# A three-branch recurrent decoder step: the row of reciprocal norms read from PSUM, and another order of the projections

## The chip, the cores and the metric

The kernel runs on one core of one Trainium2 chip. The metric is device time in microseconds (us) of one execution, and less is better. The core's engines work at the same time, each through its own instructions in order: PE (TensorE, matmuls; PEld is its weight load), DVE (VectorE), ACT (ScalarE), POOL (GpSimd) and SP (SyncE, which here only issues DMAs). Semaphores make one engine wait for another. PE writes to PSUM, which DVE and ACT can read; everything else lies in SBUF.

## The reference, cut to what matters

One layer is applied to a prompt of 2048 tokens with 16 learned tokens in front, and to 8 samples of 8 tokens (80 rows in all beside the prompt):

```
h    = rms_norm(x, norm_w)                    # x * rsqrt(mean(x*x)) * norm_w
proj = h @ w_in                               # 1024 -> 5648 + 3*1024 columns
A: q,k,v = conv(width 4) -> silu;  gated delta rule in chunks -> RMSNorm * silu(z)
B: q,k,v, input and forget gates;  mLSTM memory in chunks     -> RMSNorm * sigmoid(o) * silu(z)
C: S5: complex diagonal scan over u, gelu, GLU                -> * silu(z)
x    = x + (sum_b sigmoid(gate_b) * (branch_b @ W_b)) @ W_out
y    = rms_norm(x, final_norm_w)
```

All of it is float32, and the final states of every branch are outputs as well. Features lie on the partitions and tokens along the free dimension, so a norm is one number for each token: a row, which has to be known on all 128 partitions.

## The kernel before, in words

**Tiles.** The tokens go through in six blocks, `BLOCKS` (L30) times 128: block 0 has 336 (the 80 rows and 256 of the prompt), blocks 1 to 4 have 384, block 5 has 256. In each block every product with 128 output features is 24 matmuls: eight input chunks, and for each of them three passes (high part by high part, high by low, low by high; L199). A weight comes in two halves of 128x512 through SP's queue (L225); ACT rounds each half to its high part `wh` (L226) and DVE subtracts it for the low part `wl` (`weights`, L188 being the helper that records every such DVE operation). There are four buffers for loaded weights and three each for `wh` and `wl`.

**Steps.** A plan names the steps of a block: `R` the rows of gates (a product with a long chain of short DVE operations behind it, tiles `rX`, `rE`, `rC`, `rW`), `C` their columns, `u0` to `u3` the S5 input projections, `s0` to `s3` the S5 scans, `d0` to `d11` the delta-rule projections with their convolution, `m0` to `m11` those of the mLSTM, `p`, `I`, `N` preparations, the triangular inverse and the mLSTM gates, `M`, `g`, `D` the chunked tiles, `F` the S5 gate products of the GLU, `X0` to `X2` the branch mixes, `E` the end of the delta rule, `S` the S5 tables (block 0 only, low priority). `:1` runs a step as far as its first yield, and `!` issues the rest behind the projection then running. `PLAN0` is the plan of block 0, `PLAN` that of the others. The order in which the plan writes the steps is their priority; a scheduler then puts the instructions of each engine in order by readiness and priority, so a moved name moves work on every engine.

**Banks.** A dense product writes a bank of the PSUM pool `pd`, which has three; the next product but two takes the same bank and must wait until it has been read out. A `u` step is read out by one ACT copy (tile `s5u`), after which it goes through a DRAM buffer `us` and comes back as `s5U` for the scan. An `m` step is read out by one ACT operation. A `d` step is read by ACT twice and then by three DVE multiply-adds (`cacc`, the convolution's taps):

```
self.act(acc[:, :T], ps, AF.Copy, scale=tap(3))              # ACT reads PSUM
for j in range(3):
    self.stt(o, src(j), tap(j), o, OP.mult, OP.add)          # DVE reads PSUM
```

In block 0 the taps read a copy in SBUF instead. All other matmuls share three banks `pr` and two banks `s5`.

**The norm of block 0.** Block 0 projects before its norm is known: the products of `R` and `u0` to `u3` run on x times norm_w, and are multiplied by the row of reciprocal norms behind it. That row is a matmul of ones with a diagonal, so it is born in a `pr` bank (`self.rstd`). `norm` copies it to an SBUF tile `rb` (L359 to L362), which `rows` (one multiply) and `s5_proj` (four multiplies, the operand read with a stride) use. From the step `norm` on, block 0 uses the finished x (`xh`, `xl`). `xt` is multiplied straight by the row in PSUM.

Of the kernel before, what the change touches and what calls it, by code (L numbers as in the profile page):

```python
# [26 lines left out]
P = 128  # L27
# [4 lines left out]
TMAX = 384  # L32
# [5 lines left out]
UNITS = 12  # L38


PLAN0 = ("R u0 u1 S u2 u3 norm m8 m7 C m6 m10 m1 m0 m4 m5 d4 m9 m2 m3 d5 m11 M0 M1 M2 d0 d3 d2 s0 s1 s2 s3 d7 d8 d9 d10 d1 "
         "d6 d11 p I N X1 g0 g1 D0 D1 g2 D2 F X2 Ud E X0 Um").split()
OUT0 = ["n"] * 19 + ["o"] * 99
PLAN = ("R C u0 u1 u2 s0:1 s1:1 u3 d0 d1 s0! s2:1 m1 m0 s1! s3:1 m2 m3 s2! d6 d2 s3! d10 d3 d4 m4 m7 m6 d7 d5 m5 d8 p d9 "
        "m9 d11 M0:2 m11 M1:2 m10 m8 M0 M1 M2 F N I g0 D0 g1 D1 g2 D2 X2 X1 E X0").split()
OUT = ["n"] * 19 + ["o"] * 99


# [5 lines left out]
GROUP = {  # L54
    "rX": "rows", "rE": "rows", "rD": "rows", "rW": "rows", "rC": "rows", "rM": "rows", "rH": "rows",
    "nacc": "acc", "nsq": "wide", "cacc": "wide", "zt": "wide", "zo": "wide", "fin": "wide", "mt": "wide",
    "macc": "wide", "rb": "wide", "s5v": "raw", "s5g": "wide", "raw": "raw", "junk": "junk",
# [49 lines left out]
class Kernel:  # L107
# [219 lines left out]
    def norm(self, g):  # L327

        T, V = g.T, self.V
        xu = [self.unit([P, 4, T], name="xt") for _ in range(2)]  # L330
        xt = [xu[k // 4][:, k % 4] for k in range(8)]
        for k in range(8):
            src = self.I["xt"][k, :, g.t0:g.t0 + T]
            if g.first:
                with self.tc.high_priority(offset=5000):
                    (self.nc.sync if k % 2 else self.nc.scalar).dma_start(xt[k], src)
            else:
                self.nc.sync.dma_start(xt[k], src)
        acc = self.temp([P, TMAX], "nacc")[:, :T]
        w = lambda k: self.vec[:, V_NW + k:V_NW + k + 1]  # L340
        if g.first:

            uh, ul = ([self.unit([P, 4, T], F32R, name="xw") for _ in range(2)] for _ in range(2))
            with self.tc.high_priority(offset=4000):
                for k in range(8):
                    self.add_square(acc, xt[k], k == 0)
                    h = uh[k // 4][:, k % 4]
                    self.act(h, xt[k], AF.Copy, scale=w(k))
                    self.stt(ul[k // 4][:, k % 4], xt[k], w(k), h, OP.mult, OP.subtract)
        else:  # L350
            for k in range(8):
                self.add_square(acc, xt[k], k == 0)
        yield
        for _ in self.rstd_row(acc, g):
            yield
        rb = self.rstd
        xh, xl = ([self.xp.tile([P, 4, TMAX], F32R, name=self.name(s), tag=s, bufs=2)[:, :, :T] for _ in range(2)]
                  for s in ("xh", "xl"))
        if g.first:  # L359
            self.rb = self.temp([P, TMAX], "rb")[:, :T]  # L360
            self.A.copy(self.rb, rb)
            self.xh, self.xl = uh, ul  # L362
        self.xn = xh, xl
        for k in range(8):
            with self.tc.high_priority(offset=3000 if g.first else 0):
                self.stt(xt[k], xt[k], w(k), rb, OP.mult, OP.mult)
                self.A.copy(xh[k // 4][:, k % 4], xt[k])
                self.tt(V if g.first and k < 4 else self.G, xl[k // 4][:, k % 4], xt[k], xh[k // 4][:, k % 4], OP.subtract)
# [1057 lines left out]
    def run(self):  # L1426
# [12 lines left out]
        for b in range(len(BLOCKS)):  # L1439
# [11 lines left out]
            steps, self.live, self.mixed = self.steps(), {"O": out}, 0  # L1451
            for w in PLAN0 if self.first else PLAN:
                late = w[-1] == "!"
# [9 lines left out]
            for w in OUT0 if self.first else OUT:  # L1463
                next(out if w == "o" else norm, None)
# [109 lines left out]
```

## Time and profile before

| what | value |
|---|---|
| runs | 2762.54, 2766.62, 2773.35 us; median 2766.62 |
| profiled execution | 2762.64 us, span 2760.9 us |
| mean granted TensorE clock | 0.98 of full |
| busy | PE 2637.4 us, DVE 2020.9, ACT 1263.0, POOL 685.9 |
| blocks by PE's first matmul of `R` | 6.5, 539.4, 1006.1, 1467.7, 1931.5, 2395.0 us |

The profile is one execution. Its page lists busy times of the engines, the chain of work that ended last, and the costliest groups of instructions. Views of the trace give more: windows (busy time of each engine in a stretch), waits (for whom an engine stood idle, and how long), timelines (each instruction with the idle time ahead of it) and tiles (all instructions that touch one buffer). The span less PE's busy time is what PE stood idle, and the windows split it by block.

### The profile page before, as it was taken

The numbers are of one execution on the slowest core, as the hardware profiler recorded it, in microseconds if no ns is written. First come the engines' busy times: TensorE is split into PE (matmuls) and PEld (weight loads), VectorE is DVE, ScalarE is ACT, GpSimd is POOL, SyncE is SP. The second block draws the span as 40 slices with busy tenths as digits, with TensorE's granted clock in tenths as the row PEclk, the third lists the DMA queues.
The fourth block names the chain that finished last, engine by engine and source line by source line (L and its number), as shares of the span: only waits on it lengthen the run. The fifth ranks groups of instructions, "written<-read, shape, count | busy, mean of one in ns | idle before, by whom it ended". The sixth has DMA issues, their size and how long they took to land.

```text
span 2760.9 us, 49716 instructions
## 1 busy us (share of the span) xinstructions
PE 2637.4 (96%) x17416; PEld 2565.8 (93%) x17416; DVE 2020.9 (73%) x4458; ACT 1263.0 (46%) x2900; POOL 685.9 (25%) x852
## 2 busy tenths in 40 slices
PE   6899799999999999999999999999999999989998
PEld 5899798989999999999999999999999999979998
DVE  7889666798864589875468887456988645788765
ACT  4354343544543454553344454345445434546444
POOL 8642233211302221221221031123014022202022
PEclk8999899999999999999999999999999999999999
DMA  5635546664443455434355534335553434565544
GB/s 151 201 115 172 145 128 190 190 184 150 115 131 99 150 171 171 142 117 118 104 168 165 175 114 128 109 108 170 177 167 108 135 95 125 174 195 153 167 146 149
DMA packets 312892, 405.36 MB, mean 147 GB/s; under 512 B 118529, under 2 KB 147969, under 8 KB 312641
## 3 DMA queue, kind: packets, MB, share of 16 engines
q1 hardware_dynamic: 299760, 384.56, 46.5%
q10 hardware_dynamic: 12880, 17.62, 1.8%
q8 instruction: 137, 2.24, 0.4%
q14 instruction: 115, 0.93, 0.1%
HBM read 370.54 MB, written 31.53 MB: 146 GB/s over the span
## 4 chain that ended last, share of the span: by engine, by line
PE 64%; DVE 6%; DMA 2%; issue 1%; ACT 1%; SPq 0%; DVEq 0%; ACTq 0%
PE pd L199 55%; PE pr L199 6%; PE s L199 2%; DVE wl L188 2%; PE pr L203 1%; DVE cacc L196 1%; DVE s5a L1257 1%; DVE s5a L188 1%; DMA s5g<-ys 0%; DMA s5w<-s5w 0%; DMA s5U<-us 0%; DMA s5t<-s5p 0%; DVE h L196 0%; ACT wh L226 0%; DVE s5g L196 0%
## 5 line engine op out<-in xcount | busy, mean ns | idle before, releaser
L226 ACT CAST wh<-w 128x512 fp32r<-128x512 f32 x1092 | 674.7, 619 | 1023.2 <-PE pd L199 839.0
L188 DVE TENSOR_TENSOR wl<-w,wh 128x512 fp32r<-128x512 f32 x1092 | 814.2, 748 | 419.1 <-ACT wh L226 391.7
L199 PE MATMUL pd<-xh,wh 128*128 128x384 f32 (+2 forms) x3272 | 1077.2, 329 | 24.9 <-DVE cacc L196 13.4
L199 PE MATMUL pd<-xh,wl 128*128 128x384 f32 (+2 forms) x3272 | 1074.4, 329 | 15.3 <-DVE wl L188 14.8
L199 PE MATMUL pd<-xl,wh 128*128 128x384 f32 (+2 forms) x3272 | 1068.8, 327 | 6.4 <-DVE xl L188 6.4
L199 PEld LDWEIGHTS pd<-xh,wh 128*128 128x128 f32 x3272 | 624.8, 191 | 33.8 <-ACT wh L226 15.0
L199 PEld LDWEIGHTS pd<-xh,wl 128*128 128x128 f32 x3272 | 623.9, 191 | 26.9 <-DVE wl L188 20.6
L199 PEld LDWEIGHTS pd<-xl,wh 128*128 128x128 f32 x3272 | 624.7, 191 | 9.0 <-DVE xl L188 7.1
L188 POOL TENSOR_TENSOR macc<-macc,mt 128x384 f32<-128x384 f32 (+2 forms) x96 | 125.6, 1308 | 453.6 <-DVE mt L196 446.7
L188 POOL TENSOR_TENSOR s5a<-s5a,s5a 128x384 f32<-128x384 f32 (+2 forms) x48 | 52.4, 1106 | 599.5 <-DVE s5a L188 555.6
L199 PE MATMUL pd<-mh,wl 128*128 128x384 f32 (+2 forms) x384 | 124.6, 328 | 0.9 <-DVE wl L188 0.9
L199 PE MATMUL pd<-mh,wh 128*128 128x384 f32 (+2 forms) x384 | 124.2, 325 | 0.8 <-ACT wh L226 0.8
L199 PE MATMUL pd<-ml,wh 128*128 128x384 f32 (+2 forms) x384 | 123.2, 323 | 0.0
L196 DVE SCALAR_TENSOR_TENSOR cacc<-pd,c,cacc 128x384 f32<-128x384 f32 (+1 forms) x180 | 103.8, 583 | 0.8
L199 PE MATMUL s<-s5U,s5w 128*128 128x96 f32 (+2 forms) x576 | 87.9, 277 | 15.4 <-DMA s5U<-us 5.2
L182 POOL COPY U<-UC 32x128 f32<-32x128 f32 x68 | 22.9, 336 | 316.9 <-ACT UC L693 314.2
L196 DVE SCALAR_TENSOR_TENSOR mt<-mt,pd 128x384 f32<-128x384 f32 (+2 forms) x96 | 50.1, 522 | 68.0 <-PE pd L199 67.6
L199 PEld LDWEIGHTS s<-s5U,s5w 128*128 128x128 f32 x576 | 79.5, 194 | 20.0 <-issue 11.2
L185 ACT ACTIVATE mt<-pd,c 128x384 f32<-128x384 f32 (+2 forms) x144 | 79.4, 551 | 2.7 <-PE pd L199 2.4
L199 PEld LDWEIGHTS pd<-mh,wl 128*128 128x128 f32 x384 | 72.1, 188 | 3.6 <-DVE wl L188 3.1
L1257 DVE TENSOR_TENSOR_SCAN s5a<-s5R,s5a,s5a 128x96 f32<-128x96 f32 (+2 forms) x192 | 69.0, 419 | 7.1 <-ACT s5a L1255 6.7
L199 PEld LDWEIGHTS pd<-mh,wh 128*128 128x128 f32 x384 | 72.4, 189 | 1.9 <-ACT wh L226 1.4
(402 smaller groups left out, 4400.9 us busy)
## 6 DMA issues: line engine op xcount, KB each, us to landing
w<-in_wi_dram SPq DMA_DIRECT2D x816, 256.0 KB
w<-in_wb_dram SPq DMA_DIRECT2D x144, 256.0 KB
s5w<-s5w SPq DMA_DIRECT2D x120, 256.0 KB
w<-in_wo_dram SPq DMA_DIRECT2D x96, 256.0 KB
s5t<-s5p SPq DMA_DIRECT2D x48, 192.0 KB
w<-in_wg_dram SPq DMA_DIRECT2D x24, 256.0 KB
xt<-in_xt_dram SPq DMA_DIRECT2D x32, 192.0 KB
h<-in_xt_dram SPq DMA_DIRECT2D x8, 768.0 KB
```

Of the source, the lines that this page charges most:

```text
L182: return eng.tensor_copy(out, in_)
L185: return self.A.activation(out, in_, f, **k)
L188: return eng.tensor_tensor(out, a, b, op=op)
L196: return self.V.scalar_tensor_tensor(out, a, s, b, op0=op0, op1=op1)
L199: return self.E.matmul(out, lhsT, rhs, start=start, stop=stop, **k)
L203: return self.E.transpose(out, in_, self.ident[:n, :n])
L226: self.A.copy(h, w)
L1257: V.tensor_tensor_scan(g[:, a, 1:1 + m], self.s5R[:, 4 * f + a:4 * f + a + 1].to_broadcast([P, m]), x[:, a, 0:m], g[:, a, 0:1], OP.mult, O ...
```

## The change

First, `rb` is no longer copied: `self.rb` is the PSUM tile itself, so its group entry and the copy go, and the five multiplies of block 0 read one operand from PSUM, whose bank is held until the last of them. Second, in `PLAN0` `d4` goes ahead of `m1`, `m5` and `m3` ahead of where they were, and `N` ahead of `I`. Third, in `PLAN` the scans' first parts `s0:1`, `s1:1` go between the first projections, with `d0` and `u3` ahead of `u2`; `d3` takes the place of `m3`, which follows it, and `d6` goes behind `d4`; `X2` stands ahead of `D2`.

```
-PLAN0 = ("R u0 u1 S u2 u3 norm m8 m7 C m6 m10 m1 m0 m4 m5 d4 m9 m2 m3 d5 m11 M0 M1 M2 d0 d3 d2 s0 s1 s2 s3 d7 d8 d9 d10 d1 "
-         "d6 d11 p I N X1 g0 g1 D0 D1 g2 D2 F X2 Ud E X0 Um").split()
+PLAN0 = ("R u0 u1 S u2 u3 norm m8 m7 C m6 m10 d4 m1 m0 m5 m4 m3 m9 m2 d5 m11 M0 M1 M2 d0 d3 d2 s0 s1 s2 s3 d7 d8 d9 d10 d1 "
+         "d6 d11 p N I X1 g0 g1 D0 D1 g2 D2 F X2 Ud E X0 Um").split()
-PLAN = ("R C u0 u1 u2 s0:1 s1:1 u3 d0 d1 s0! s2:1 m1 m0 s1! s3:1 m2 m3 s2! d6 d2 s3! d10 d3 d4 m4 m7 m6 d7 d5 m5 d8 p d9 "
-        "m9 d11 M0:2 m11 M1:2 m10 m8 M0 M1 M2 F N I g0 D0 g1 D1 g2 D2 X2 X1 E X0").split()
+PLAN = ("R C u0 u1 s0:1 d0 s1:1 u3 u2 d1 s0! s2:1 m1 m0 s1! s3:1 m2 d3 m3 s2! d2 s3! d10 d4 d6 m4 m7 m6 d7 d5 m5 d8 p d9 "
+        "m9 d11 M0:2 m11 M1:2 m10 m8 M0 M1 M2 F N I g0 D0 g1 D1 g2 X2 D2 X1 E X0").split()
-    "macc": "wide", "rb": "wide", "s5v": "raw", "s5g": "wide", "raw": "raw", "junk": "junk",
+    "macc": "wide", "s5v": "raw", "s5g": "wide", "raw": "raw", "junk": "junk",
         if g.first:
-            self.rb = self.temp([P, TMAX], "rb")[:, :T]
-            self.A.copy(self.rb, rb)
+            self.rb = rb
             self.xh, self.xl = uh, ul
```

On PE, blocks 1 to 4 ran `R u0 u1 u2 u3 d0 d1 m1 m0 C m2 m3 d6 d2 d10 d3 d4 m4` with the scans in between, and now run `R u0 u1 d0 u3 u2 d1 m1 m0 C m2 d3 m3 d2 d10 d4 d6 m4`; from `d9` to the end of a block the steps come in the same order. The two swaps `N I` and `X2 D2` leave nearly every instruction where it was. Line numbers behind the copy are one less than before.

In block 0, DVE's rows at the multiplies by the norm row are these before (`rX` of `rows`, `s5u` and `s5v` of the S5 projections, `wl` of `m8` ahead, `xl` the low part of x):

```order
L188 TENSOR_TENSOR wl_229_988<-w_227_986,wh_228_987 128x512
L188 TENSOR_TENSOR rX_97_383<-rX_97_383,rb_46_210 128x336
L188 TENSOR_TENSOR s5u_118_485<-s5u_118_485,rb_46_210 128x4x84
L188 TENSOR_TENSOR s5v_126_526<-s5v_126_526,rb_46_210 128x4x84
L188 TENSOR_TENSOR s5u_216_939<-s5u_216_939,rb_46_210 128x4x84
L188 TENSOR_TENSOR xl_44_208<-xt_21_127,xh_42_206 128x336
L188 TENSOR_TENSOR wl_232_1006<-w_230_1004,wh_231_1005 128x512
```

and now:

```order
L188 TENSOR_TENSOR rX_96_381<-rX_96_381,pr_41_204 128x336
L188 TENSOR_TENSOR s5u_117_483<-s5u_117_483,pr_41_204 128x4x84
L188 TENSOR_TENSOR s5v_125_524<-s5v_125_524,pr_41_204 128x4x84
L188 TENSOR_TENSOR wl_228_986<-w_226_984,wh_227_985 128x512
L188 TENSOR_TENSOR s5u_215_937<-s5u_215_937,pr_41_204 128x4x84
L188 TENSOR_TENSOR xl_44_208<-xt_21_127,xh_42_206 128x336
L188 TENSOR_TENSOR wl_231_1004<-w_229_1002,wh_230_1003 128x512
```

The operand `rb_46` has become `pr_41`, the bank that `xt` is multiplied by, and the first `wl` of `m8` has moved behind three of the multiplies.

At the start of block 3, DVE's rows around the eight residual additions `h` of the block before were these (`wl_3517` and `wl_3520` are the halves of `d0`, `wl_3527` the first of `d1`; `rC`, `rE` are rows of `R`):

```order
L196 SCALAR_TENSOR_TENSOR rC_3438_16806<-rC_3438_16806,rW_3437_16805 64x384
L188 TENSOR_TENSOR wl_3517_17154<-w_3515_17152,wh_3516_17153 128x512
L196 SCALAR_TENSOR_TENSOR rC_3438_16806<-rC_3438_16806,rW_3437_16805 64x384
L196 SCALAR_TENSOR_TENSOR rC_3438_16806<-rC_3438_16806,rE_3435_16803 64x384 x2
L196 SCALAR_TENSOR_TENSOR h_3351_16388<-h_3351_16388,c_1_91,pr_3423_16743 128x384 x4
L196 SCALAR_TENSOR_TENSOR h_3352_16389<-h_3352_16389,c_1_91,pr_3423_16743 128x384 x4
L192 TENSOR_SCALAR rE_3439_16824<-rC_3438_16806,c_9_110 64x384
L188 TENSOR_TENSOR wl_3520_17172<-w_3518_17170,wh_3519_17171 128x512
L188 TENSOR_TENSOR wl_3527_17202<-w_3525_17200,wh_3526_17201 128x512
```

and now (`cacc_3489` is the convolution of `d0`, `wl_3518` and `wl_3521` the halves of `u2`):

```order
L188 TENSOR_TENSOR wl_3518_17160<-w_3516_17158,wh_3517_17159 128x512
L196 SCALAR_TENSOR_TENSOR rC_3437_16804<-rC_3437_16804,rW_3436_16803 64x384
L196 SCALAR_TENSOR_TENSOR cacc_3489_17047<-pd_3481_17008,c_6_105,cacc_3489_17047 128x384
L196 SCALAR_TENSOR_TENSOR rC_3437_16804<-rC_3437_16804,rE_3434_16801 64x384
L196 SCALAR_TENSOR_TENSOR cacc_3489_17047<-pd_3481_17008,c_6_105,cacc_3489_17047 128x384 x2
L196 SCALAR_TENSOR_TENSOR rC_3437_16804<-rC_3437_16804,rE_3434_16801 64x384
L196 SCALAR_TENSOR_TENSOR h_3350_16386<-h_3350_16386,c_1_91,pr_3422_16741 128x384 x4
L196 SCALAR_TENSOR_TENSOR h_3351_16387<-h_3351_16387,c_1_91,pr_3422_16741 128x384 x4
L188 TENSOR_TENSOR wl_3521_17178<-w_3519_17176,wh_3520_17177 128x512
L192 TENSOR_SCALAR rE_3438_16822<-rC_3437_16804,c_9_110 64x384
L188 TENSOR_TENSOR wl_3526_17200<-w_3524_17198,wh_3525_17199 128x512
```

The three multiply-adds of `d0`, which stood 14, 19 and 24 rows behind the first `h`, stand ahead of it, and the second half behind `h` is that of `u2`.

In block 5, ACT's rows from the eight output DMAs on (`wh_5675` is the second half of `m1`, `wh_5679` and `wh_5682` are those of `m0`, `pd_5632` is the bank of `d0`, `pd_5642` that of `d1`) were these:

```order
L1393 DMA out_yt_dram<-h_5469_26798 128x384 x4
L1393 DMA out_yt_dram<-h_5470_26799 128x384 x4
L226 CAST wh_5675_27755<-w_5674_27754 128x512
L226 CAST wh_5679_27775<-w_5678_27774 128x512
L244 COPY pd_5632_27559<-c_12_116 128x3
L244 COPY pd_5642_27607<-c_12_116 128x3
L226 CAST wh_5682_27793<-w_5681_27792 128x512
L572 COPY c_11_115<-pd_5632_27559 128x3
L185 ACTIVATE cacc_5640_27598<-pd_5632_27559,c_6_105 128x256
L572 COPY c_11_115<-pd_5642_27607 128x3
L185 ACTIVATE cacc_5650_27646<-pd_5642_27607,c_6_105 128x256
```

and now (`wh_5674` of `m1`, `wh_5678` of `m0`, `pd_5633` the bank of `u2`, `pd_5641` that of `d1`):

```order
L1392 DMA out_yt_dram<-h_5468_26796 128x384 x4
L1392 DMA out_yt_dram<-h_5469_26797 128x384 x4
L226 CAST wh_5674_27753<-w_5673_27752 128x512
L226 CAST wh_5678_27773<-w_5677_27772 128x512
L1201 COPY s5u_5640_27602<-pd_5633_27565 128x4x64
L244 COPY pd_5641_27605<-c_12_116 128x3
L571 COPY c_11_115<-pd_5641_27605 128x3
L185 ACTIVATE cacc_5649_27644<-pd_5641_27605,c_6_105 128x256
```

The operations on `d0`'s bank have gone from behind the DMAs (they stand seven rows and more ahead of them now), and one copy of `u2`'s bank stands there instead.

## Rows read from the trace of the kernel before

**Rows 1.** The page: busy us (share of the span) xinstructions.

```profile
PE 2637.4 (96%) x17416; PEld 2565.8 (93%) x17416; DVE 2020.9 (73%) x4458; ACT 1263.0 (46%) x2900; POOL 685.9 (25%) x852
```

**Rows 2.** Windows by block: stretch, length, busy us (instructions) of five engines, clock, DMA.

```profile
0.00:539.40 539.40, 483.76 (x3100) 448.92 (x3101) 413.89 (x955) 228.23 (x537) 236.54 (x382) 0.94 0.53 162
539.40:1006.10 466.70, 457.98 (x2903) 450.96 (x2902) 334.70 (x711) 213.07 (x482) 97.82 (x99) 0.99 0.46 139
1006.10:1467.70 461.60, 454.60 (x2902) 446.84 (x2901) 333.97 (x710) 213.83 (x482) 96.95 (x99) 1.00 0.47 140
1467.70:1931.50 463.80, 455.47 (x2901) 447.86 (x2900) 334.00 (x710) 214.30 (x482) 97.07 (x99) 1.00 0.46 139
1931.50:2395.00 463.50, 455.59 (x2900) 448.05 (x2899) 330.24 (x709) 212.60 (x482) 93.74 (x99) 1.00 0.46 139
2395.00:2760.90 365.90, 330.05 (x2720) 323.21 (x2718) 274.09 (x664) 180.94 (x435) 63.78 (x74) 0.96 0.55 163
```

**Rows 3.** Waits of PE, block 0: engine, line, awaited; us, times, longest.

```profile
PE pd L199 <- DVE wl L188: 11.1, 6, 5.9
...
PE pd L199 <- DVE xl L188: 6.4, 2, 6.0
...
PE pr L203 <- DVE s5X L188: 2.9, 2, 1.9
```

**Rows 4.** Tile rb: count, min/median/max ns, first and last start us.

```profile
L188 DVE TENSOR_TENSOR s5u<-s5u,rb x2: 769/1118/1467, 40.4 to 42.5; 128x336 f32<-128x336 f32 x2
L188 DVE TENSOR_TENSOR s5v<-s5v,rb x2: 1326/1388/1450, 41.1 to 51.3; 128x336 f32<-128x336 f32 x2
...
L188 DVE TENSOR_TENSOR rX<-rX,rb x1: 518/518/518, 40.0 to 40.0; 128x336 f32<-128x336 f32 x1
```

**Rows 5.** Tile xt, 30 to 45 us: one operand from PSUM.

```profile
L196 DVE SCALAR_TENSOR_TENSOR xt<-xt,c,pr x8: 559/559/565, 35.0 to 38.3; 128x336 f32<-128x336 f32 x8
```

**Rows 6.** Tile nacc, 5 to 60 us: both operands in SBUF.

```profile
L188 DVE TENSOR_TENSOR nacc<-nacc,nsq x7: 436/500/524, 11.5 to 18.6; 128x336 f32<-128x336 f32 x7
```

**Rows 7.** Timeline of POOL, 88 to 104 us: start, length, instruction, [idle before, releaser].

```profile
101.10 0.71 POOL L188 TENSOR_TENSOR s5xy<-s5t 128x8 f32<-128x8 f32 x1 [10.72 <-DVE rW L188]
```

**Rows 8.** Timeline of DVE, 128 to 141.5 us.

```profile
137.99 2.08 DVE L188 TENSOR_TENSOR Z<-ml,c 128x64 f32<-128x64 f32 x4 [6.10 <-POOL ml L188]
```

**Rows 9.** Timeline of PE, 134 to 141.5 us.

```profile
140.72 0.65 PE L199 MATMUL pd<-xh,wl 128*128 128x336 f32 x1 [5.87 <-DVE wl L188]
```

**Rows 10.** Waits of PE, blocks 1 to 4.

```profile
PE pd L199 <- DVE cacc L196: 7.8, 4, 3.6
PE s L199 <- DMA s5U<-us: 5.1, 3, 2.3
PE pd L199 <- DVE wl L188: 2.6, 7, 0.7
PE pr L203 <- DVE rX L196: 2.5, 3, 0.9
```

**Rows 11.** Windows at the start of block 3.

```profile
1467.70:1489.00 21.30, 21.30 (x130) 21.04 (x129) 16.57 (x39) 10.35 (x19) 0.00 (x0) 1.00 0.50 146
1489.00:1505.80 16.80, 15.41 (x90) 14.85 (x89) 16.43 (x34) 6.75 (x16) 0.00 (x0) 1.00 0.87 274
1505.80:1545.00 39.20, 35.51 (x214) 34.23 (x215) 38.44 (x77) 17.67 (x52) 5.75 (x4) 1.00 0.55 163
```

**Rows 12.** The page: the conv's multiply-adds.

```profile
L196 DVE SCALAR_TENSOR_TENSOR cacc<-pd,c,cacc 128x384 f32<-128x384 f32 (+1 forms) x180 | 103.8, 583 | 0.8
```

**Rows 13.** Waits of PE, block 5.

```profile
PE pd L199 <- DVE cacc L196: 5.6, 1, 5.6
...
PE s L199 <- DMA s5w<-s5w: 2.7, 2, 1.6
...
PE pd L199 <- ACT wh L226: 2.3, 1, 2.3
```

**Rows 14.** Timeline of ACT, 2414 to 2433 us.

```profile
2415.59 7.59 ACTq L1393 DMA_DIRECT2D out_yt_dram<-h  x8
```

## The prediction

> **What bounds the kernel now.** I read the page's totals first: PE is busy 2637.4 us of 2760.9, 96% [rows 1], so nothing can be won but what PE stands idle, 123.5 us. The windows by block divide it [rows 2]: each block's length less PE's busy time is 55.6 us in block 0, then 8.7, 7.0, 8.3 and 7.9, and 35.9 in block 5 (its tail included). Blocks 1 to 4, two thirds of the time, hold only 32 us of it, and the reader should see that no order of theirs can be worth more than that. In block 0 and block 5 the granted clock is 0.94 and 0.96 on average, so for part of them PE ran at 1.2 instead of 2.4 GHz.
>
> Then the waits of PE, one query for each kind of block. In blocks 1 to 4 it waited 7.8 us for `cacc`, once in each block: the convolution of `d0`, whose bank `m0` takes. It waited 5.1 us for S5's input to come back from DRAM, 2.6 for low weights and 2.5 for `rX`, the rows behind `C` [rows 10]. Block 5 has the same wait on `cacc` in one piece of 5.6 us, 2.3 us for a high weight and 2.7 for S5's weights [rows 13]. In block 0 it waited 11.1 us for low weights and 6.4 for `xl`, most of it in pieces of 5.9 and 6.0 [rows 3]. Nearly all of these end on DVE, which is the second thing to see: at the start of block 3 DVE is busy 16.43 us of 16.80 and 38.44 of 39.20, while the 21.3 us ahead leave it 4.7 idle [rows 11].
>
> **The norm row in PSUM.** The five multiplies by `rb` take 2.24, 2.78 and 0.52 us, 5.53 in all [rows 4]: two of `s5u`, two of `s5v`, one of `rX`. A multiply of 336 columns with both operands in SBUF took 0.50 us in a quiet stretch [rows 6], so four of the five are two to three times as long as the work needs. The multiply of `xt` with one operand from PSUM, same partitions and columns, took 0.56 in all eight instances, in the same crowded part [rows 5]. No row shows a strided read from PSUM. Bounds: each at 0.56 is 2.80, a gain of 2.7; each at the longest present multiply, 1.47, is 7.3, a loss of 1.8. I take 0.65 each, near [rows 5], a gain of 2.3.
>
> The Trainium skill, SBUF — State Buffer, "Who interferes with whom", says that a Vector instruction with two SBUF inputs contends with a GpSimd instruction that reads SBUF, and one with at most one SBUF input does not; the trace agrees, with 0.56 against up to 1.47 [rows 4, 5]. Against the change speaks the skill's VectorE: DVE Perf Modes, "Rules for kernel authors": copy from PSUM to SBUF first if many operations follow. Its Perfetto Trace Analysis, "Optimizing Scalar/DVE Operations", gives about 125 ns of access for PSUM against 60 for SBUF, by which five reads would lose 0.3 us (an estimate), and the sum would be 7.7 and not 10.
>
> The copy that goes was ACT's and nobody's bound. The bank held longer is one of three, until the last multiply at 51.3 us [rows 4]; I cost it at nothing, because the dense products have banks of their own and two of `pr` remain, and if a product of the S5 tables wanted the third, it would wait beside dense work. Of 2.3 us on DVE I count 2.0 on PE, since PE stands on `xl` and low weights right there [rows 3].
>
> **The order of block 0.** `m3` and `d4` come earlier and fill the two waits on `s5X`, 2.9 us [rows 3]. But what follows is bound elsewhere: POOL's long chain begins at 101.10, after 10.72 us of waiting for DVE's `rW` [rows 7]; its product `ml` is what DVE waits 6.10 us for in front of `Z` [rows 8], and behind `Z` stands the low weight that costs PE 5.87 us [rows 9]. PE arriving earlier only waits longer there, unless POOL begins earlier, and POOL begins earlier by DVE's gain. DVE gains about the 2.0 above and perhaps a little by order, so I book 0.5 for the order: 2.5 for block 0. Bounds: 6 won if `Z` no longer waits, 1 lost if the stall moves ahead into `d0`.
>
> **Blocks 1 to 4.** With `d0` ahead of `u2`, the bank that `m0` takes was last `u2`'s, read out by one ACT copy instead of a convolution; `d0`'s bank goes to `d1`, two projections after `d0`. So the 7.8 us on `cacc` go from this place. What is late next: DVE. The three multiply-adds, 3 x 0.583 = 1.75 us [rows 12], move out of the full stretch to ahead of `h`, into the 4.7 us of idle [rows 11]. They delay `h` by what does not fit between the rows, which I put at 0.8, so DVE comes out of it 1.0 us earlier in a block, and PE cannot gain more than DVE does while low weights bound it: the second half of `m0`'s weight, with a row of `rE` now in front, takes over part of the wait. I take 0.75 in each, 3.0. Bounds: all of [rows 10], 18, won; and 1.75 a block, 7, lost, if the moved convolution lands on the path.
>
> `d3` for `m3`, `m3` for `d6` and `d6` behind `d4` exchange steps of equal length (24 matmuls, two weight halves); they shift convolutions by a step and I cost them at nothing, with DVE's idle as cover. On SP's queue `u2`'s row to DRAM is issued some ten weight loads later, behind those of `m0` and `m2`; its reader `s2` comes five products after that, so I leave the 5.1 us on S5's input where it is. If that cover is gone, it doubles. `X2` ahead of `D2` and `N` ahead of `I` are worth nothing: the rows of every engine stay, or nearly.
>
> **Block 5.** Here `d0`'s readers on ACT stood behind eight output DMAs, 7.59 us of issuing [rows 14], and now they are ahead of them. `m0` needs only `u2`'s copy, which comes right behind its own first cast, so the 5.6 us go [rows 13]. The 2.3 on the high weight of `m1` stay, since that cast is still behind the DMAs. The load of S5's second weights now stands behind eight weight loads instead of six, and DVE has to bring `m0`'s second half; I give 1.1 of the 5.6 back: 4.5. Bounds: 8 won (with the 2.3 or the 2.7 also gone), 3 lost (all kept, and 2.7 doubled).
>
> **The sum.** 2.5 + 3.0 + 4.5 = 10.0 us. Against the profiled execution (span 2760.9 and 1.74 around it, 2762.64) this gives 2752.6; that execution lies 4.0 under the median of the runs, 2766.62, so a median would be 2756.6. I forecast 2755.
>
> **The rivals.** *The waits only move.* DVE is full where PE waits [rows 11], the first stall of block 0 is POOL's, and S5's loads cap each block: then only block 0's 2.0 is left, and the time is 2761 to 2765, say 2763. For it: PE's idle is small and is spread over many releasers. Against: block 5's wait hangs on ACT, which is busy only 46% [rows 1].
>
> *More goes than I book.* The waits on `cacc`, 7.8 + 5.6, go whole, `rX` 2.5 with them, and block 0 gives 6: 21.9, so 2741 to 2745, with a bit more if shorter stalls leave PE at 2.4 GHz for longer in blocks 0 and 5. For it: the bank is free by one ACT copy. Against: the full DVE.
>
> *Slower: the convolution of `d0` comes in the way.* Its 1.75 us stand ahead of `h`, and the second half of `u2`'s weight stands behind the eight `h`. If that half is not there when `u2`'s first 12 matmuls end, PE waits where it did not before. Price: 1.75 in five blocks, 8.8, and the S5 loads that shift with `u2`, 5.1 + 2.7 again, 16.6 in all, with nothing of the waits won: 2762.6 + 16.6 = 2779, by the median 2783, so 2781. It decides once `h` is delayed by more than the 1.75. For it: [rows 11], 16.43 of 16.80. Against: 4.7 us idle just ahead.
>
> *The swap in the title does nothing:* that holds in all four cases, and changes no number.
>
> **How the numbers follow.** The forecast (5 to 15 us won) has 0.50, the waits that move 0.18, the larger gain 0.22, the slower case 0.10. A measurement of this kernel can tell about 0.5%, 13.8 us, from no change: under 2752.8 is faster, above 2780.4 slower. A third of the forecast's range lies under it, 0.17, and all of the larger gain: 0.38 faster. Of the slower case 0.07 lies above. 0.55 is left for the same. The range goes from 2742, the middle of the larger gain, to 2770, which leaves most of the slower case out; the forecast's own is 2749 to 2762.
>
> **What would show it.** Multiplies by `pr` near 0.6 us, and `xl` ended for PE some 2 us earlier at 45; a wait in front of `Z` still near 6 us; no PE wait on `cacc` in front of `m0` in blocks 1 to 5, and in its place low weights of `m0` under 1 us; S5's input about 5 us as before; block lengths in the windows of 1 to 4 shorter by 0.5 to 1 us each, block 5's by 4 to 5. I am wrong if the PSUM multiplies take over 1 us, if waits on low weights in blocks 1 to 4 grow by more than `cacc` gives, or if block 0 changes by more than 6 us.

## The result, and the profile after

The changed kernel takes 2734.38 us, the median of four runs (2732.65 to 2739.41), where four of the kernel before took 2764.58 (2758.48 to 2773.35). The ratio is 0.9895, 95% interval 0.9881 to 0.9910: about 29 us by the ratio and 30 by the medians, three times the 10 that were forecast, and below the stated range. The profiled execution is the slowest of the four, 2739.41 us with a span of 2737.6, so the two traces differ by 23.3 us only.

The windows by block of the changed kernel (stretch, length, busy us and instructions of PE, PEld, DVE, ACT, POOL, granted clock, DMA share, GB/s), each from `R` to the next `R`:

```profile
0.00:539.70 539.70, 483.31 (x3101) 448.25 (x3102) 409.45 (x955) 229.75 (x536) 229.97 (x382) 0.94 0.54 162
539.70:999.80 460.10, 455.61 (x2901) 448.38 (x2901) 332.85 (x711) 213.74 (x482) 95.90 (x99) 1.00 0.47 141
999.80:1457.80 458.00, 454.26 (x2903) 446.79 (x2902) 333.11 (x710) 213.57 (x482) 95.78 (x99) 1.00 0.47 141
1457.80:1919.20 461.40, 455.51 (x2901) 448.23 (x2901) 331.78 (x710) 213.78 (x482) 95.85 (x99) 1.00 0.47 140
1919.20:2379.50 460.30, 453.84 (x2899) 446.67 (x2899) 329.30 (x709) 211.84 (x482) 93.64 (x99) 1.00 0.47 140
2379.50:2737.60 358.10, 327.90 (x2719) 320.01 (x2718) 271.88 (x664) 180.23 (x435) 67.01 (x74) 0.97 0.56 166
```

Beside [rows 2], block 0 is as long as it was (539.7 against 539.4), blocks 1 to 4 are shorter by 6.6, 3.6, 2.4 and 3.2 us, and block 5 by 7.8. Between these two traces all of the gain is made in blocks 1 to 5, 15.8 and 7.8 us, where 3.0 and 4.5 had been booked. Both traces turn out to be unusual in places, which the table under "The baseline" below shows.

What PE waited for in blocks 1 to 4 (engine, line, awaited: us, times, longest):

```profile
PE pd L199 <- DVE wl L188: 5.5, 11, 0.8
PE s L199 <- issue: 2.3, 1, 2.3
PE s L199 <- DMA s5U<-us: 1.7, 1, 1.7
PE s L199 <- DMA w<-in_wi_dram: 1.0, 1, 1.0
```

The 7.8 us on `cacc` and the 2.5 on `rX` [rows 10] are gone, and low weights took over 2.9 more, in pieces under 1 us. The waits of `s2` are the last three of these, 5.0 us. Before they were 6.8: the 5.1 on S5's input [rows 10] and 1.7 that ended with a weight load. In block 5:

```profile
PE s L199 <- DMA s5w<-s5w: 2.9, 3, 1.1
PE pd L199 <- DVE cacc L196: 2.6, 1, 2.6
PE pd L199 <- DVE wl L188: 2.3, 4, 1.4
PE pd L199 <- ACT wh L226: 1.6, 1, 1.6
```

The 5.6 us on `cacc` [rows 13] have become 2.6: that is now `m2`, waiting for the convolution of `d1`.

Block 0 looks the same by length only. The multiplies by the row in PSUM (count, min/median/max ns, first and last start) did better than the row they were priced by:

```profile
L188 DVE TENSOR_TENSOR s5u<-s5u,pr x2: 492/493/494, 39.4 to 46.9; 128x336 f32<-128x336 f32 x2
L188 DVE TENSOR_TENSOR s5v<-s5v,pr x2: 493/496/499, 39.8 to 51.2; 128x336 f32<-128x336 f32 x2
L188 DVE TENSOR_TENSOR rX<-rX,pr x1: 493/493/493, 38.9 to 38.9; 128x336 f32<-128x336 f32 x1
```

Each takes 0.49 us, the strided ones too, 2.5 in all against 5.5 [rows 4]. But here is DVE's timeline right behind the first three (start, length, instruction):

```profile
39.77 0.49 DVE L188 TENSOR_TENSOR s5v<-s5v,pr 128x336 f32<-128x336 f32 x1
40.19 6.78 DVE L188 TENSOR_TENSOR wl<-w,wh 128x512 fp32r<-128x512 f32 x1
46.89 0.49 DVE L188 TENSOR_TENSOR s5u<-s5u,pr 128x336 f32<-128x336 f32 x1
47.30 0.50 DVE L188 TENSOR_TENSOR xl<-xt,xh 128x336 fp32r<-128x336 f32 x1
```

and POOL's in the same place:

```profile
39.92 2.61 POOL L188 TENSOR_TENSOR xl<-xt,xh 128x336 fp32r<-128x336 f32 x3
42.50 2.35 POOL L188 TENSOR_TENSOR s5m<-s5cf,s5B 128x256 f32<-128x256 f32 x4
44.81 0.89 POOL L188 TENSOR_TENSOR xl<-xt,xh 128x336 fp32r<-128x336 f32 x1
45.64 0.09 POOL L565 MEMSET raw<- 128x3 f32 x1
45.70 0.72 POOL L188 TENSOR_TENSOR s5Bb<-s5m,s5m 128x256 f32<-128x256 f32 x1
```

The first low weight of `m8`, which took 1.2 us before, took 6.78. It subtracts two SBUF operands, and POOL ran operations that read SBUF from 39.92 to 46.42, with nothing between them but one memset of 0.09 us; the weight ended at 46.97, 0.55 us behind POOL's run. PE paid for it:

```profile
PE pd L199 <- DVE wl L188: 9.7, 10, 3.3
...
PE pd L199 <- DVE xl L188: 8.4, 1, 8.4
```

It waited 8.4 us for `xl`, where [rows 3] has 6.0 for the same piece. DVE saved 3.0 us on the multiplies and lost 5.5 in one instruction among them. It did not end up late for that: POOL's run was over sooner, and what came next on DVE ran undisturbed. From the first multiply of `xt` to the reciprocal of `rD` DVE took 19.4 us instead of 20.4. What was late was this one weight and the `xl` behind it, and those are what PE stood waiting for.

### The profile page after: what moved, and what is told of

Same layout as the page of the kernel before. It is cut to its first block, busy times and chain, and to the rows that moved or that the text cites. A ratio compares the mean times of both kernels' runs of the same rounds, so it can differ in the third digit from the quotient of the medians.

```text
span 2737.6 us, 49691 instructions
## 1 busy us (share of the span) xinstructions
PE 2630.4 (96%) x17416; PEld 2558.3 (93%) x17416; DVE 2008.4 (73%) x4458; ACT 1262.9 (46%) x2899; POOL 678.1 (25%) x852
## 4 chain that ended last, share of the span: by engine, by line
PE 80%; DVE 10%; DMA 4%; issue 2%; POOL 2%; ACT 1%; SPq 1%; ACTq 0%; DVEq 0%; POOLq 0%
PE pd L199 66%; PE pr L199 9%; PE s L199 3%; DVE wl L188 3%; PE pr L203 2%; DVE s5a L1256 1%; DMA w<-in_wo_dram 1%; DVE s5a L188 1%; DVE cacc L196 1%; ACT wh L226 1%; POOL s5xy L188 0%; DMA s5U<-us 0%; DMA out_s_mlc_dram<-st 0%; DMA s5g<-ys 0%; DMA s5w<-s5w 0%
## 5 line engine op out<-in xcount | busy, mean ns | idle before, releaser
L199 PEld LDWEIGHTS pd<-ml,wh 128*128 128x128 f32 x384 | 72.8, 190 | 0.1
```

The lines of the kernel that those rows point to most:

```text
L199: return self.E.matmul(out, lhsT, rhs, start=start, stop=stop, **k)
```

## The experiments

Times are medians, ratios are to the kernel before, with 95% intervals from runs on the same chip.

**The norm row alone.** The entry of `rb` in the table of buffer groups goes as well.

```
-            self.rb = self.temp([P, TMAX], "rb")[:, :T]
-            self.A.copy(self.rb, rb)
+            self.rb = rb
```

> Only the norm row stays in PSUM; both plans are as before. Theory A (the gain of the multiplies is lost again, because the first low weight of m8 lands behind them and runs against POOL's chain of reading operations): the five multiplies take 0.49 us each, 2.5 in all instead of 5.5, but that low weight takes 5 to 7 us instead of 1.2, PE waits over 8 us for xl, and the time is within 3 us of before. Rival B (the PSUM reads are a clean gain and the other order of block 0 spoils it): the low weight stays near 1.2 us, m8 ends 2 us earlier, and the time falls by 2 to 5 us.

2760.22 us against 2762.55, ratio 0.9991 (0.9981 to 1.0002). The low weight took 6.78 us and PE waited 8.4 for `xl`: theory A in its mechanism. In time it is 2.3 us, which the interval does not separate from nothing.

**The plan of blocks 1 to 5 alone.** The `PLAN` lines of the change, nothing else.

> Only the plan of blocks 1 to 5 changes. Theory A (nearly the whole gain is made at the starts of blocks 1 to 5): the time falls by 22 to 28 us, block 1 is some 6 us shorter, blocks 2 to 4 some 3 us each, block 5 some 8, block 0 as before. Rival B (block 0 gives a third of the median's gain): it falls by 14 to 18 us.

2740.12 us, 0.9920 (0.9905 to 0.9934): 22.4 us, in theory A's range. From the read-out of one `R` to the next, blocks 1 to 4 were 460.4, 458.6, 461.2 and 459.0 us, where the first trace of the kernel before has 466.6, 461.6, 463.9 and 462.3. Block 0, whose code is that of before, showed something its first trace had not:

```profile
39.35 6.47 DVE L188 TENSOR_TENSOR s5u<-s5u,rb 128x336 f32<-128x336 f32 x1
```

A multiply by the copied row took 6.47 us, again under POOL's run, and PE waited 9.4 us for `xl`. The five other kernels that copy the row (below) show the same instruction at 6.47 or 6.48. The trace that the prediction was worked out from, with the longest of these at 1.47 [rows 4], was the exception.

**The plan of block 0 alone.** The `PLAN0` lines, nothing else.

> Only the plan of block 0 changes; the norm row is copied as before. Theory A (a stall that goes comes back at the next one bound by POOL or by a round trip): block 0 ends within 2 us of before. Rival B (the order of block 0 is worth something and the long low weight of m8 hid it): block 0 is 3 to 6 us shorter and the wait in front of Z is no longer.

2758.85 us, 0.9985 (0.9973 to 0.9998): 3.7 us, at the lower end of rival B, with an interval from under 1 to 7 us. Runs went from 2748.94 to 2764.42, and the profiled one was the fastest, with block 0 some 8 us shorter than before, so the trace flatters it. In it `Z` waited 0.78 us for `ml` instead of 6.10 [rows 8], and the longest wait of PE behind it was 0.5 us, in `d0`, instead of 5.9 in `d3` [rows 9]. The norm row alone had left both as they were, 6.64 and 6.37. So it is the order of block 0 that takes this stall away, and rival B is nearer.

**The front part of the plan.**

```
-PLAN = ("R C u0 u1 u2 s0:1 s1:1 u3 d0 d1 ...
+PLAN = ("R C u0 u1 s0:1 d0 s1:1 u3 u2 d1 ...
```

> Of the plan of blocks 1 to 5 only the front part changes (s0 and s1 between the first projections, d0 and u3 ahead of u2); d3, m3, d6 and X2 stay where they were. Theory A (the bank of d0 and the convolution of d0 are what counts): it gives most of what the whole plan gives, 15 us or more, and m0's wait on cacc is gone in all five blocks. Rival B (the second half, d3 for m3 and d6 behind d4, carries a good part because S5's scans then find their data): it gives under 12 us, and the waits in front of s2 stay at 5 us in sum.

2744.53 us, 0.9941 (0.9918 to 0.9964): 18.0 us of the whole plan's 22.4, though the interval reaches from 10 to 23. `m0` no longer waited for `cacc` in any block. The waits of `s2` were 4.6 us, as rival B had said, but the time is theory A's by the median.

**The second part of the plan.**

```
-"... m2 m3 s2! d6 d2 s3! d10 d3 d4 m4 ..."
+"... m2 d3 m3 s2! d2 s3! d10 d4 d6 m4 ..."
```

> Of the plan of blocks 1 to 5 only the second part changes (d3 for m3, m3 behind it, d6 behind d4); u2 stays ahead of d0. The whole plan gave 22 us and the front part alone 18. Theory A (the front part frees DVE, and the second part only helps where that has been done): this gives under 3 us, with m0's waits on cacc as before, 7.8 us in blocks 1 to 4 and 5.6 in block 5. Rival B (the two parts add up): 4 to 6 us.

2754.85 us, 0.9969 (0.9957 to 0.9982): 7.7 us, more than either theory gave. The waits of PE in blocks 1 to 4:

```profile
PE pd L199 <- DVE cacc L196: 7.7, 4, 3.5
PE pd L199 <- DVE wl L188: 3.1, 7, 0.8
PE pr L203 <- DVE rX L196: 2.5, 3, 0.9
```

The three rows of [rows 10] on DVE are nearly unchanged, 7.7, 3.1 and 2.5 us. What is missing is the wait of `s2`: of 6.8 us in blocks 1 to 4, 0.7 is left. In block 3 the first DMA that loads this input for `s2` was issued 65.7 us behind the row product's read-out instead of 67.1; on SP's queue one weight load now stands behind two loads of S5's weights and not ahead of them. That this is the reason was not tested by itself. With the front part as well, part of the wait is back (3.7 us with the whole plan), which fits the two parts, 18.0 and 7.7, giving 22.4 together; but the intervals would allow a plain sum too.

**The bank alone.** Both plans as before; in blocks 1 to 5 the convolution of `d0` reads a copy (`first_d` is 4, the number that `d0` hands to this function).

```
+            if n == self.first_d:
+                self.A.copy(raw[:, 0:T + 3], self.lead[:, 13:16 + T])
+                parts.append((acc[:, :T], lambda j: raw[:, j:j + T]))
+            else:
+                parts.append((acc[:, :T], lambda j, t=self.lead: t[:, 13 + j:13 + j + T]))
```

> Both plans are as before, but in blocks 1 to 5 the convolution of d0 reads an SBUF copy that ACT makes, so the bank that m0 takes is free without DVE; DVE's work and its order stay. Theory A (the front part of the plan gains because the convolution leaves DVE's full stretch; the bank is only where the wait showed): m0 waits for its low weights instead, the rows for C stay late, and the time falls by under 6 us, a third of what the front part gave. Rival B (the bank alone is it): m0's waits on cacc go in all five blocks with nothing in their place, and 12 us or more are won.

2757.39 us, 0.9988 (0.9976 to 0.9999): 5.2 us. The waits on `cacc` are gone from blocks 1 to 4, and this is in their place:

```profile
PE pd L199 <- DVE wl L188: 11.9, 11, 2.3
```

2.6 us of waiting for low weights have become 11.9, and from read-out to read-out blocks 1 to 4 took 1851.3 us together, no less than the 1851.1 with the norm row alone, where their code is that of before. This is theory A: freeing the bank does not help there while the convolution stays in DVE's full stretch. One thing was not kept equal: with both operands in SBUF, the third multiply-add took 1.42 us in each of these blocks instead of 0.6, right ahead of the weight that `m0` waits for, so 0.8 of each wait of 2.3 comes from the copy. Without that the bank alone might be worth some 3 us in these four blocks, an estimate from four times 0.8, where the plan gives about 12. In block 5 it is otherwise:

```profile
PE pd L199 <- ACT raw L185: 3.4, 1, 3.4
```

The copy is ACT's, and `m0` waits 3.4 us for ACT where it had waited 5.6 for DVE. Block 5 took 356.4 us instead of 362.4, so the whole gain of this run lies in block 5.

**All of `xl` on DVE.** The changed kernel with

```
-                self.tt(V if g.first and k < 4 else self.G, xl[k // 4][:, k % 4], ...
+                self.tt(V if g.first else self.G, xl[k // 4][:, k % 4], ...
```

> The changed kernel, with all eight low parts of x in block 0 subtracted on DVE instead of four on DVE and four on POOL. Theory A (POOL's back-to-back reading operations kept one DVE operation for 6.8 us from its second SBUF operand): POOL's run of reading operations is some 3 us shorter, the long DVE operation ends with it at about 3.5 us instead of 6.8, PE's wait for xl falls from 8.4 to 5 to 6.5 us, and the time falls by 1 to 4 us against the changed kernel. Rival B (the operation is long for a reason of its own, a semaphore or the queue): it stays at 6.8 us, four more subtractions on DVE cost 2 us, and the kernel is slower than the changed one by 1 to 3 us.

2740.03 us, 0.9920 (0.9902 to 0.9939), against 0.9893 for the changed kernel beside it: 8 us slower. Neither theory had both halves. DVE's timeline, and then POOL's:

```profile
39.25 0.93 DVE L188 TENSOR_TENSOR wl<-w,wh 128x512 fp32r<-128x512 f32 x1
...
40.95 1.10 DVE L188 TENSOR_TENSOR wl<-w,wh 128x512 fp32r<-128x512 f32 x1
41.97 3.69 DVE L188 TENSOR_TENSOR xl<-xt,xh 128x336 fp32r<-128x336 f32 x4
```

```profile
39.02 3.51 POOL L188 TENSOR_TENSOR s5m<-s5cf,s5B 128x256 f32<-128x256 f32 x4
```

The long weight is gone: DVE and POOL slowed each other instead, with weights at 0.93 and 1.10 us, four low parts at 0.92 each, and POOL's four products at 0.88 instead of the 0.59 that they took in the changed kernel's POOL rows above. The waits of PE in block 0:

```profile
PE pd L199 <- DVE wl L188: 7.4, 7, 3.1
PE pd L199 <- ACT ml L185: 5.7, 1, 5.7
...
PE pd L199 <- DVE xl L188: 2.9, 2, 2.6
...
PE pr L203 <- POOL s5n L188: 2.6, 1, 2.6
```

`xl` fell from 8.4 to 2.9 us, but the wait on a bank read by ACT (`ml`) rose from 3.2 us in the changed kernel's second trace to 5.7, that on low weights from 5.3 to 7.4, and one of 2.6 on the S5 tables (`s5n`) is new. From the read-out of one `R` to the next block 0 took 528.6 us against 519.6 there. Taking a wait out at the start of block 0 did not shorten the block.

**All of `xl` on POOL.** The same line with `self.tt(self.G, ...)`.

> The changed kernel with all eight low parts of x in block 0 subtracted on POOL instead of four, so that its run of reading operations is four longer (0.87 us each as they ran undisturbed). Theory A (POOL's run keeps DVE's second SBUF operand away until it ends): the long low weight of m8 grows from 6.8 us to about 10, and PE's wait moves from xl to that weight. Rival B (DVE's operation is long for a reason of its own): it stays at 6.8 us, and since DVE has four subtractions less, what is behind it comes 2 us earlier.

2738.11 us, 0.9942 (0.9926 to 0.9958). The long weight of DVE, and the last of POOL's run of reading operations:

```profile
40.66 8.60 DVE L188 TENSOR_TENSOR wl<-w,wh 128x512 fp32r<-128x512 f32 x1
```

```profile
46.92 1.79 POOL L188 TENSOR_TENSOR s5m<-s5cf,s5B 128x256 f32<-128x256 f32 x3
```

It took 8.60 us and ended at 49.26, where POOL's run ended at 48.71. This is the second low weight of `m8`; the first slipped through in 1.05. The long instruction grew with POOL's run, and ends with it, 0.55 us behind in both kernels, and PE waited 7.5 us for that weight. This is theory A, though 10 had been said. The time is 11 us above the 2727.10 that the kernel of the experiment on `X2` below took on the same chip.

**The changed kernel again.**

> The changed kernel again, beside the run above and with a second profile. Theory A (block 0 comes out differently from execution to execution, since POOL and DVE race for their operands there, and blocks 1 to 5 do not): 0.9895 of before within 0.002, blocks 1 to 5 within 1 us each of the first profile, and block 0 elsewhere by 2 us or more. Rival B (the plan's new order is as stable as the old one everywhere): block 0 within 1 us too.

2731.83 us, 0.9893 (0.9872 to 0.9913). Its window of block 0:

```profile
0.00:533.30 533.30, 483.27 (x3100) 449.07 (x3101) 407.04 (x955) 229.81 (x536) 230.22 (x382) 0.95 0.53 164
```

533.3 us, where the first trace has 539.7: 6.4 of the 7.2 us between the two spans lie in block 0. This is theory A, but for one detail: blocks 1 and 2 differ by 1.2 and 1.8 us between the two traces, so they are not stable within 1.

**`X2` behind `D2` again.** In the changed kernel `g2 X2 D2` becomes `g2 D2 X2`.

> The changed kernel with X2 put back behind D2. Theory A (this part of the change changes no engine's order): the same as the changed kernel, 0.989 of before within 0.002, blocks 1 to 5 within 1 us each. Rival B (it carries part of what blocks 1 to 4 gained): slower than the changed kernel by 4 us or more.

2727.10 us where before took 2752.45 on that chip, 0.9904 (0.9886 to 0.9922): the same ratio as the changed kernel, which was not run on that chip itself. Blocks 1 to 4 were 458.5, 458.4, 461.0 and 456.8, up to 2.2 us under the first trace, about the spread seen above. This swap, which the prediction calls the one in the title, does nothing that these runs can tell.

**The norm row copied again.** The changed kernel with the two lines of the copy put back.

> The changed kernel with the norm row copied to SBUF again. Theory A (the 3 us that the PSUM reads save on DVE go into the wait for POOL's reading operations, which then catches a low weight instead of a multiply): one multiply by the copied row takes over 6 us, PE waits some 9 us for xl, and the time is 0 to 3 us above the changed kernel's. Rival B (the PSUM read is worth its 3 us of DVE in full, because DVE is full there): 3 to 6 us above.

2733.45 us, 0.9919 (0.9905 to 0.9934). On the same chip the kernel with `X2` moved, as good as the changed one, took 2727.10, so the PSUM row is worth 6.3 us by these medians and 4 by the two ratios; the two intervals overlap. One multiply took 6.48 us and PE waited 9.4 us for `xl`, as theory A had it, but the time is rival B's. Between 2.3 us alone and 6.3 here, its size stays open.

## Why the prediction was wrong

**The direction and the places were right, the sizes were not.** The prediction's four terms were 2.0 for the norm row, 0.5 for block 0's order, 3.0 for blocks 1 to 4 and 4.5 for block 5. The runs give 2.3 to 6.3, 3.7, and 22.4 for the last two together. So the step that failed is the pair "I take 0.75 in each" and "4.5", booked 7.5: most of the shortfall, 15 us of some 20, lies there, about 12 us being won in blocks 1 to 4 and some 8 in block 5 (the table under "The baseline"). The rest is block 0, booked 2.5.

**A premise: "nothing can be won but what PE stands idle".** It bounded everything, and it is not so. Between the two traces PE's idle time fell by 16.3 us, and its busy time fell by 7.0, from 2637.4 to 2630.4 us for the same products. Part of that is the clock, in the third error below.

**Blocks 1 to 4, the first error: how much DVE is freed.** The prediction let DVE come out 1.0 us earlier, 1.75 for the convolution less 0.8 for the delay of `h`. The stretch of block 3 from the first `h` to the last `rX` before `C`, in the kernel before:

```profile
1489.00:1511.05 22.05, 19.83 (x114) 18.97 (x112) 21.56 (x42) 8.41 (x18) 1.40 (x1) 1.00 0.73 231
```

and in the changed kernel:

```profile
1479.60:1499.10 19.50, 19.02 (x109) 18.50 (x108) 19.09 (x39) 7.02 (x15) 1.39 (x1) 1.00 0.81 253
```

DVE's busy time is the third of the busy figures: 21.56 and 19.09 us. The stretch is 2.5 us shorter, not 1.75, mainly because one low weight fewer, 0.68 us, stands in it too, which the sum left out. (Two other differences nearly cancel: a row of `rE` took 1.38 us before and 0.55 now, and another of 0.64 has come in.) And `h` began 17.0 us behind the row product's read-out instead of 16.6, a delay of 0.4 where 0.8 was booked: most of the three multiply-adds fitted into pauses of DVE. So DVE was 2.1 us ahead, and PE, which follows it here, took that: `C` in block 3 came 2.0 us earlier. The rule "PE cannot gain more than DVE does" held at this point; its number was half of what it should have been. The experiment on the bank alone shows that rule from the other side. The rest of the 3 us in a block comes behind `C` and was not taken apart; the wait of PE on S5's `s5a`, 1.1 us in three blocks before, is gone too.

**The second error: "I leave the 5.1 us on S5's input where it is".** The swap of `d3`, `m3` and `d6` was costed at nothing as an exchange of equal steps. Alone it gave 7.7 us, and nearly all of the wait on S5's input went with it. The prediction looked at SP's queue for `u2`'s row on its way out, and not for the loads of `s2`.

**The third: a wait was priced at its length.** In block 1 PE's one wait of 3.56 us on `cacc` was followed by a stretch at a lower clock; here is the kernel before, and then the changed one, where `m0` waits only 0.2, for a low weight:

```profile
580.00:590.00 10.00, 10.00 (x48) 9.96 (x49) 9.76 (x18) 3.69 (x14) 3.65 (x1) 0.73 0.34 104
```

```profile
576.00:582.00 6.00, 5.79 (x36) 5.25 (x34) 5.87 (x11) 2.33 (x5) 1.38 (x1) 1.00 0.31 95
```

0.73 is a mean over stretches at 1.2 and 2.4 GHz; PE was busy throughout, and `m0` took 6.96 us against 4.83. Block 1 gained 6.6 us between the two traces, of which 3.4 are the wait and 2.1 the clock. The clock's part varies from execution to execution. With the norm row alone, blocks 1 to 5 have the code of before, and behind the same wait of 3.57 us the trace shows

```profile
580.00:590.00 10.00, 10.00 (x54) 9.97 (x55) 9.94 (x19) 4.22 (x14) 5.67 (x1) 0.85 0.43 129
```

Here `m0` took 5.87 us, and 5.98 in the traces of the plan of block 0 alone and of the second part, so 1.0 to 2.1 us go with this wait. In block 5 the same holds in part, the stretch with `m0` of before and after:

```profile
2425.00:2440.00 15.00, 9.35 (x63) 9.09 (x62) 14.68 (x39) 5.34 (x21) 1.69 (x2) 0.66 0.28 86
```

```profile
2410.00:2425.00 15.00, 12.42 (x81) 12.07 (x81) 14.65 (x35) 6.27 (x18) 1.69 (x2) 0.79 0.50 144
```

0.66 against 0.79. The prediction put this into a rival, "with a bit more", without a number, although [rows 2] showed the clock.

**Block 5** lost the 5.6 on `cacc` as forecast, with 2.6 coming back at `m2`, and kept 1.6 of the 2.3 on the high weight. The wait on S5's weights did not double with the two more weight loads ahead, 2.9 us against 2.7. With the clock the block is 7.8 us shorter between the two traces.

**Block 0.** "`xl` ended for PE some 2 us earlier" is wrong: PE's wait for it is 8.4 us instead of 6.0 in the trace, and ended at 47.85 us, not 45. The prediction priced the multiplies well and said that two-operand instructions suffer under POOL, but took from it only a gain for those that change, not that the next one in line would suffer in their place. Its "two to three times as long as the work needs" was also read too high: the first `s5u`, 0.77 us, is one and a half times the 0.50, and with POOL idle, in the traces of the kernels that copy the row, `s5u` and `s5v` took 0.74. And "POOL begins earlier by DVE's gain" put the order at 0.5. With the order alone, POOL waited 3.50 us for `rW` instead of 10.72 [rows 7], and `Z`'s wait fell to 0.78. In the first trace of the changed kernel `Z` waited 1.48 us, not 6, and the stall moved into `d0` at 1.8 us, a small one, as the bound had it. Why the other order shortens POOL's wait was not tested.

**The baseline.** The sum was made against one trace and the forecast set between it and a median of three. Block 0 differs by 6 us between two traces of one kernel, so part of the difference between 23 us by traces and 29 by runs is which executions were profiled. Here are the stretches from read-out to read-out of `R`, in us (block 5 to the end of the span):

| trace | block 0 | blocks 1 to 4 | block 5 |
|---|---|---|---|
| before | 524.7 | 1854.4 | 362.3 |
| norm row alone | 526.5 | 1851.1 | 362.4 |
| plan of block 0 alone | 517.0 | 1850.7 | 359.7 |
| plan of blocks 1 to 5 alone | 529.5 | 1839.2 | 352.4 |
| front part of that plan | 526.4 | 1841.1 | 355.6 |
| second part of that plan | 529.2 | 1845.3 | 360.6 |
| bank alone | 528.9 | 1851.3 | 356.4 |
| changed | 525.8 | 1838.6 | 354.6 |
| changed, second trace | 519.6 | 1839.0 | 353.3 |

The first trace has the shortest block 0 of the five with that code (the others are the two parts, the whole plan of blocks 1 to 5 and the bank), and the longest blocks 1 to 4 of the first three rows, which share their code. So the plan gives about 12 us in blocks 1 to 4, 3 in each, rather than the 15.8 between the first two traces; and block 0, which seems to give nothing there, is 525.8 and 519.6 us against 526 to 530 in the other four.

The rival "more goes than I book", at 0.22, named the right waits, and its 21.9 us were still too few, since it too took waits at their length. The slower rival did not show: in blocks 1 to 4 of the changed kernel PE has no wait of 0.25 us or more ahead of `m0`, so none at `u2`.

## What to carry to other kernels

When an engine is full just where another waits for it, count every instruction that leaves the full stretch between the two points that matter, and not only the one the change is about; then look at which pauses ahead can take them. Idle time of the busiest engine is no bound on the gain while its clock can change: look at the busy time at the lower clock too. A wait freed at one place (a bank, an operand) is worth something only if the engine behind it has time, so try the release alone before believing in it. And take several executions of the kernel before: one that happens to miss a collision makes the wrong baseline.

## What the runs showed of the hardware

When DVE and POOL wanted SBUF operands at once, it went in one of two ways here. In the kernel with all of `xl` on DVE, and in the trace of the kernel before, they slowed each other, both to between two fifths and three quarters of their speed. In the eleven other traces, one DVE instruction with two SBUF operands was kept out until POOL's run of reading instructions ended: 6.47 to 6.78 us for an instruction that takes 0.7 undisturbed, and 8.60 when the run was made longer. The multiplies with the norm row in PSUM took 0.49 to 0.50 us in the same stretch, never more. What decides between the two ways was not found; the code of block 0 of the kernel before showed both.

The place of the strided operand mattered too. With POOL idle, the strided multiplies by the copied row took 0.74 us, both operands in SBUF, and those by the row in PSUM 0.49, as long as a plain multiply of the same columns. Why was not tested.
